# The first load of a layer norm cut into three strided transfers, with a 64-byte write per DMA engine between the first two

## The chip, the cores and the metric

One core of one Trainium2 chip. The metric is the device time of one execution in microseconds, as a median over executions. All runs told here are of the state "fast", with a granted clock of 1.0. Ratios are the mean time of one kernel's fast runs over that of the other's fast runs of the same rounds on the same chip, so they are not quite the ratio of the medians that are quoted beside them.

## The reference

Condensed:

```python
def reference(x, residual, gamma, beta, eps):        # x, residual: 16 x 1024 x 512, float32
    z = x + residual
    mean = np.mean(z, axis=-1, keepdims=True)
    var = np.var(z, axis=-1, keepdims=True)
    return (gamma * (z - mean) / np.sqrt(var + eps) + beta).astype(np.float32)
```

Two tensors of 33.5 MB are read and one is written: 100.7 MB through the DMA engines.

## The kernel before

Every row is 512 floats (2 KB). A partition holds 128 rows, and `x32+16` in the plan means: rows 32 to 47 of each of the 128 partitions. GpSimd adds x and the residual into `rbuf`, ScalarE makes mean and variance, VectorE normalizes into `zbuf`, and the result is stored from there. All large transfers are issued by SyncE on one queue, in the order of the plan. The first two are moved ahead of the barrier at which the engines meet at the start.

```python
PLAN = """
x0+8 r0+8 x8+8 r8+8 x16+16 r16+16 x32+16 r32+16 x48+16
o0+16 r48+16 o16+16 x64+16 r64+16 x80+16 o32+16 r80+16
x96+16 r96+16 o48+8 o56+8 r112+8 x112+8 r120+8 x120+8
o64+16 o80+16 o96+16 o112+8 o120+4 o124+4
"""
EARLY = 2
# ... buffers, semaphores, gamma and beta ...
    def move(out, in_, s):
        i = nc.sync.dma_start(out=out, in_=in_).then_inc(s, 16)
        if len(first) < EARLY:
            first.append(i.ins)
    for kind, lo, n in moves:
        if kind == "x":
            # ... wait until the buffer's rows have been stored ...
            move(part(zbuf, Z_ROWS, lo, n), dram(xf, lo, n), sx[loads_x.index((lo, n))])
        elif kind == "r":
            # ... wait until the buffer's rows have been used ...
            move(part(rbuf, R_ROWS, lo, n), dram(rf, lo, n), sr[loads_r.index((lo, n))])
        else:
            if lo + n > seen:
                nc.sync.wait_ge(s_out, lo + n)
                seen = lo + n
            move(dram(of, lo, n), part(zbuf, Z_ROWS, lo, n), so[stores.index((lo, n))])
# ... GpSimd waits for x and r (16 on each load's semaphore), then adds ...
# ... at the end, `first` is moved into the opening, ahead of the start barrier ...
```

Of the kernel before, what the change touches and what calls it, by code (L numbers as in the profile page):

```python
# [8 lines left out]
FP32 = mybir.dt.float32  # L9
# [5 lines left out]
Z_ROWS = 64  # L15
# [16 lines left out]
Z_TURNS = Z_ROWS // TURN  # L32


EARLY = 2


@with_exitstack
def kernel(
# [9 lines left out]
    nc = tc.nc  # L49
    P = nc.NUM_PARTITIONS  # L50
    xf = x.flatten_outer_dims()
    rf = residual.flatten_outer_dims()
    of = out.flatten_outer_dims()
# [14 lines left out]
    def of_kind(kind):  # L68
        found = [(lo, n) for k, lo, n in moves if k == kind]
        assert sum(n for _, n in found) == total  # L70
        return found

    def dram(t, lo, n):

        b0 = lo - lo % BLOCK
        v = t[P * b0 : P * (b0 + BLOCK), :].rearrange("(p j) d -> p j d", p=P)
        return v[:, lo - b0 : lo - b0 + n, :].rearrange("p a b -> p (a b)")

    zbuf = nc.alloc_sbuf_tensor("zbuf", [P, Z_ROWS * D], FP32)
    rbuf = nc.alloc_sbuf_tensor("rbuf", [P, R_ROWS * D], FP32)  # L80
    gb_row = nc.alloc_sbuf_tensor("gb_row", [1, 2 * D], FP32)
    ones = nc.alloc_sbuf_tensor("ones", [1, P], FP32)
    eps_t = nc.alloc_sbuf_tensor("eps_t", [P, 1], FP32)
    nm, ssq, std, rstd = (
        nc.alloc_sbuf_tensor(name, [P, R_ROWS], FP32) for name in ("nm", "ssq", "std", "rstd")
# [11 lines left out]
    def sem(name):  # L97
        s = nc.alloc_semaphore(name)
        sems.append(s)
        return s  # L100

    loads_x, loads_r, stores = of_kind("x"), of_kind("r"), of_kind("o")
    sx = [sem(f"sx{c}") for c in range(len(loads_x))]
    sr = [sem(f"sr{c}") for c in range(len(loads_r))]
    s_gb = [sem(f"gb{k}") for k in range(2)]
    s_const = sem("const")
    s_pe = sem("pe")
    s_sum, s_mean, s_ssq, s_std = (
        [sem(f"{name}{j}") for j in range(R_TURNS)] for name in ("sum", "mean", "ssq", "std")
# [7 lines left out]
    def part(buf, size, lo, n):  # L117
        assert lo % size + n <= size
        return buf[:, (lo % size) * D : (lo % size + n) * D]
# [17 lines left out]
    first = []  # L137

    def move(out, in_, s):
        i = nc.sync.dma_start(out=out, in_=in_).then_inc(s, 16)  # L140
        if len(first) < EARLY:
            first.append(i.ins)

    gone = 0
    for kind, lo, n in moves:
        if kind == "x":
            while gone < len(stores) and stores[gone][0] < lo + n - Z_ROWS:
                nc.sync.wait_ge(so[gone], 16)
                gone += 1
            move(part(zbuf, Z_ROWS, lo, n), dram(xf, lo, n), sx[loads_x.index((lo, n))])  # L150
        elif kind == "r":
            if lo + n > R_ROWS:
                last = (lo + n - R_ROWS) // TURN - 1
                nc.sync.wait_ge(s_rstd[last % Z_TURNS], last // Z_TURNS + 1)
            move(part(rbuf, R_ROWS, lo, n), dram(rf, lo, n), sr[loads_r.index((lo, n))])
        else:
            if lo + n > seen:
                nc.sync.wait_ge(s_out, lo + n)
                seen = lo + n
            move(dram(of, lo, n), part(zbuf, Z_ROWS, lo, n), so[stores.index((lo, n))])  # L160
# [9 lines left out]
    landed = {"x": 0, "r": 0}  # L170
    lo = 0
    for n in ADDS:
        for key, loads, s in (("x", loads_x, sx), ("r", loads_r, sr)):
            while landed[key] < len(loads) and loads[landed[key]][0] < lo + n:
                nc.gpsimd.wait_ge(s[landed[key]], 16)  # L175
                landed[key] += 1
        z = part(rbuf, R_ROWS, lo, n)
        nc.gpsimd.tensor_tensor(  # L178
            out=z, in0=part(zbuf, Z_ROWS, lo, n), in1=z, op=ALU.add
        ).then_inc(s_sum[lo // TURN % R_TURNS], 1)  # L180
        lo += n
# [131 lines left out]
```

## Time and profile before

| | before |
|---|---|
| time, median of 3 runs | 238.48 us (238.36 to 238.83) |
| span of the profiled run | 236.7 us |
| busy: VectorE, ScalarE, GpSimd | 75%, 78%, 61% |
| the one large queue | 99.4% of 16 DMA engines' span |

The last row is the one to read: the 16 DMA engines are the bound. The lines of the profile stand in the prediction. The timeline of the start shows when SyncE issues transfers (start, duration, both in us), the timeline of GpSimd when it can add for the first time, which is when the first loads of x and of the residual have landed on every engine:

```profile
0.00 0.38 SPq L140 DMA_DIRECT2D zbuf<-in_x_dram  x1
...
0.43 0.42 SPq L140 DMA_DIRECT2D rbuf<-in_residual_dram  x1
1.92 0.33 SPq L140 DMA_DIRECT2D zbuf<-in_x_dram  x1
```

```profile
12.29 4.49 POOL L178 TENSOR_TENSOR rbuf<-zbuf,rbuf 128x2048 f32<-128x2048 f32 x1 [11.85 <-DMA rbuf<-in_residual_dram]
```

### The profile page before, as it was taken

To read this page: it belongs to the slowest core of one execution; us is meant where nothing else is said; L and a number is where in the kernel's file an instruction comes from. 1 tells how busy PE (TensorE), PEld (TensorE's weight loads), DVE (VectorE), ACT (ScalarE), POOL (GpSimd) and SP (SyncE) were. 2 spreads that over 40 slices of the span, in tenths; PEclk is the share of its full clock that TensorE was granted. 3 is DMA by queue.
4 is the path that set the end of the run, shared out by engine and by line. 5 is a ranking of instruction groups with operands and counts; after the bars stand their busy time and mean duration, and the time that the engine had idled before them with its cause. 6 is when DMAs were issued, how large, how long until landed. Compare 5 with 4: busy or idle time off the path is not lost.

```text
span 236.7 us, 1000 instructions
## 1 busy us (share of the span) xinstructions
PE 3.8 (2%) x4; PEld 1.2 (0%) x4; DVE 177.2 (75%) x290; ACT 183.8 (78%) x545; POOL 144.0 (61%) x36
## 2 busy tenths in 40 slices
PE   0600000000000000000000000000000000000000
PEld 0100000000000000000000000000000000000000
DVE  0001999629999999599980999809999999999950
ACT  2019997299999996999909998099999999999600
POOL 0098920999799307993079920899799798800000
DMA  8999999999999999999999999999999999999997
GB/s 310 443 426 432 426 443 443 443 443 443 410 388 443 443 443 432 426 393 432 443 443 443 443 438 421 415 421 432 429 424 435 426 432 440 439 432 443 438 390 324
DMA packets 4469, 100.68 MB, mean 425 GB/s; under 512 B 498, under 2 KB 498, under 8 KB 500
## 3 DMA queue, kind: packets, MB, share of 16 engines
q1 hardware_dynamic: 4464, 100.67, 99.4%
q14 instruction: 1, 0.01, 0.0%
q10 hardware_dynamic: 4, 0.00, 0.0%
HBM read 67.11 MB, written 33.55 MB: 425 GB/s over the span
## 4 chain that ended last, share of the span: by engine, by line
ACT 48%; DMA 35%; POOL 6%; DVE 4%; issue 1%; SPq 1%; ACTq 0%; DVEq 0%; POOLq 0%
DMA rbuf<-in_residual_dram 35%; ACT junk_s L211 25%; ACT junk_m L201 21%; POOL rbuf L178 6%; DVE zbuf L239 3%; ACT std L220 2%; DVE zbuf L253 1%; SPq L140 1%; DVE rstd L247 0%; ACTq L194 0%; DVEq L231 0%; POOLq L175 0%; ACTq L199 0%; ACTq L195 0%
## 5 line engine op out<-in xcount | busy, mean ns | idle before, releaser
L178 POOL TENSOR_TENSOR rbuf<-zbuf,rbuf 128x2048 f32<-128x2048 f32 x32 | 143.7, 4521 | 62.2 <-DMA rbuf<-in_residual_dram 60.0
L239 DVE SCALAR_TENSOR_TENSOR zbuf<-rbuf,nm,gamma_p 128x512 f32<-128x512 f32 x128 | 87.1, 743 | 47.8 <-ACT std L220 47.8
L201 ACT ACTIVATE junk_m<-rbuf 128x512 f32<-128x512 f32 x128 | 74.2, 580 | 34.0 <-POOL rbuf L178 33.7
L211 ACT ACTIVATE junk_s<-rbuf,nm 128x512 f32<-128x512 f32 x128 | 88.8, 694 | 1.0
L253 DVE SCALAR_TENSOR_TENSOR zbuf<-zbuf,rstd,beta_p 128x512 f32<-128x512 f32 x128 | 87.1, 744 | 1.1
L211 ACT ACTIVATION_READ_ACCUMULATOR junk_s<-rbuf,nm 128x1 f32 x128 | 23.9, 187 | 0.0
L201 ACT ACTIVATION_READ_ACCUMULATOR junk_m<-rbuf 128x1 f32 x128 | 23.8, 186 | 0.0
L220 ACT ACTIVATE std<-ssq,eps_t 128x4 f32<-128x4 f32 x32 | 9.5, 297 | 1.0
L247 DVE RECIPROCAL rstd<-std 128x4 f32<-128x4 f32 x32 | 5.5, 171 | 0.0
L192 ACT ACT_TABLE_LOAD x1 | 1.3, 1283 | 2.7 <-PEq L60 2.7
L131 PE MATMUL gamma_p<-gb_row,ones 1*128 1x512 f32 x2 | 2.0, 1122 | 6.6 <-DMA gb_row<-in_gamma_dram 6.6
L131 PE MATMUL beta_p<-gb_row,ones 1*128 1x512 f32 x2 | 1.9, 1056 | 0.0
L126 DVE MEMSET ones<- 1x128 f32 x1 | 0.2, 165 | 2.0 <-PEq L60 2.0
L131 PEld LDWEIGHTS beta_p<-gb_row,ones 1*128 1x128 f32 x2 | 0.7, 332 | 1.0 <-DMA gb_row<-in_beta_dram 0.5
L131 PEld LDWEIGHTS gamma_p<-gb_row,ones 1*128 1x128 f32 x2 | 0.5, 306 | 6.6 <-issue 6.6
L294 POOL MEMSET const-float32-0.0<- 128x1 f32 x1 | 0.1, 98 | 0.2 <-issue 0.2
L294 POOL MEMSET const-bfloat16-1.0<- 128x1 bf16 x1 | 0.1, 101 | 0.0
L294 POOL MEMSET const-uint8-127<- 128x1 uint8 x1 | 0.1, 101 | 0.0
L294 POOL MEMSET const-float32-1.0<- 128x1 f32 x1 | 0.1, 98 | 0.0
L127 DVE MEMSET eps_t<- 128x1 f32 x1 | 0.1, 59 | 0.0
## 6 DMA issues: line engine op xcount, KB each, us to landing
zbuf<-in_x_dram SPq DMA_DIRECT2D x6, 4096.0 KB, 28.9
rbuf<-in_residual_dram SPq DMA_DIRECT2D x6, 4096.0 KB, 21.2
out_dram<-zbuf SPq DMA_DIRECT2D x6, 4096.0 KB, 31.0
zbuf<-in_x_dram SPq DMA_DIRECT2D x4, 2048.0 KB, 14.9
rbuf<-in_residual_dram SPq DMA_DIRECT2D x4, 2048.0 KB, 14.0
out_dram<-zbuf SPq DMA_DIRECT2D x3, 2048.0 KB, 22.5
out_dram<-zbuf SPq DMA_DIRECT2D x2, 1024.0 KB, 10.0
gb_row<-in_gamma_dram ACTq DMA_DIRECT2D x1, 2.0 KB
```

Source lines behind the costliest of these rows:

```text
L126: nc.vector.memset(ones[:, :], 1.0).then_inc(s_const, 1)
L131: nc.tensor.matmul(dest[:, :], ones[:, :], gb_row[:, k * D : (k + 1) * D], start=True, stop=True).then_inc(s_pe, 1)
L140: i = nc.sync.dma_start(out=out, in_=in_).then_inc(s, 16)
L178: nc.gpsimd.tensor_tensor(out=z, in0=part(zbuf, Z_ROWS, lo, n), in1=z, op=ALU.add).then_inc(s_sum[lo // TURN % R_TURNS], 1)
L192: act.preload_act_table_set("sqrt_and_others")
L201: i = act.activation(out=junk_m[k][:, :], in_=part(rbuf, R_ROWS, r, 1), func=ACT.Identity, scale=-inv_d, accum_out=column(nm, r),)
L211: i = act.activation(out=junk_s[k][:, :], in_=part(rbuf, R_ROWS, r, 1), func=ACT.Square, bias=column(nm, r), accum_out=column(ssq, r),)
L220: act.activation(out=column(std, rows[0], TURN), in_=column(ssq, rows[0], TURN), func=ACT.Sqrt, bias=eps_t[:, 0:1], scale=inv_d,).then_inc ...
L239: dve.scalar_tensor_tensor(out=part(zbuf, Z_ROWS, r, 1), in0=part(rbuf, R_ROWS, r, 1), scalar=column(nm, r), in1=gamma_p[:, :], op0=ALU.ad ...
L247: dve.reciprocal(out=column(rstd, rows[0], TURN), in_=column(std, rows[0], TURN)).then_inc(s_rstd[j], 1)
L253: i = dve.scalar_tensor_tensor(out=z, in0=z, scalar=column(rstd, r), in1=beta_p[:, :], op0=ALU.mult, op1=ALU.add,)
L294: nc = _bacc.Bacc("TRN2", target_bir_lowering=False, num_devices=1)
```

## The change

The evident intent: engines should start on a short first piece, and the cost of the first write to the output, a stall near 69 us, should be paid at the start, where the engines wait for their first read anyway. The residual's first load falls out of the opening, as the list of early instructions is filled by the pieces. The diff, with line positions left out and two declarations (the scratch tile and the two semaphores) cut:

```diff
-EARLY = 2
+TOUCH = 16
+FIRST = [(0, 4), (2, 4), (1, 2)]
 ...
-        if len(first) < EARLY:
+        if len(first) < len(FIRST) + 3:
             first.append(i.ins)
 ...
-            move(part(zbuf, Z_ROWS, lo, n), dram(xf, lo, n), sx[loads_x.index((lo, n))])
+            for a, step in FIRST if lo == 0 else [(0, 1)]:
+                move(
+                    part(zbuf, Z_ROWS, lo, n)[a::step, :],
+                    dram(xf, lo, n)[a::step, :],
+                    sx[loads_x.index((lo, n))],
+                )
+                if len(first) == 1:
+                    first.append(nc.vector.memset(zeros[:, :], 0.0).then_inc(s_zero, 1).ins)
+                    first.append(nc.sync.wait_ge(s_zero, 1).ins)
+                    move(dram(of, 0, 1)[::8, 0:TOUCH], zeros[::8, :], s_touch)
 ...
             if lo + n > seen:
+                if lo == 0:
+                    nc.sync.wait_ge(s_touch, 16)
                 nc.sync.wait_ge(s_out, lo + n)
 ...
-                nc.gpsimd.wait_ge(s[landed[key]], 16)
+                pieces = len(FIRST) if key == "x" and landed[key] == 0 else 1
+                nc.gpsimd.wait_ge(s[landed[key]], 16 * pieces)
```

The pieces are partitions 0, 4, 8 ... (32 of them), 2, 6, 10 ... (32) and all odd ones (64): two, two and four packets of 16 KB for each engine.

## The prediction

> **What bounds the kernel now.** I began with the page's second and third parts, because they say at once whether an engine or the transfers carry the time.
>
> ```profile
> DMA  8999999999999999999999999999999999999997
> GB/s 310 443 426 432 426 443 443 443 443 443 410 388 443 443 443 432 426 393 432 443 443 443 443 438 421 415 421 432 429 424 435 426 432 440 439 432 443 438 390 324
> q1 hardware_dynamic: 4464, 100.67, 99.4%
> HBM read 67.11 MB, written 33.55 MB: 425 GB/s over the span
> ```
>
> The reader is to see that all loads and stores go through one queue and that its packets fill 99.4% of the 16 DMA engines' span of 236.7 us; only the first and the last slice (5.9 us each) are weaker. VectorE (75%), ScalarE (78%) and GpSimd (61%) all idle more. The page's chain of work that ended last puts 48% on ScalarE, but it ends with the last compute instruction, not with the last store. The timeline of the end shows the difference:
>
> ```profile
> 216.75 11.81 SPq L140 DMA_DIRECT2D out_dram<-zbuf  x3
> 225.48 2.72 DVE L253 SCALAR_TENSOR_TENSOR zbuf<-zbuf,rstd,beta_p 128x512 f32<-128x512 f32 x4
> ```
>
> Compute ends at 225.48 + 2.72 = 228.20 us, the last store is issued at 228.2 us, and the transfers run on to 236.7 us. I put the queue's issue times beside the landing times of the trace's records: from the fourth load on, every transfer is issued at least 5 us before the queue would run dry. So the kernel is a continuous stream with a head (before the first packet) and a few stalls inside; a stall that goes shortens the whole by its length, until some 5 us are won.
>
> Next I looked for the stalls: windows of half a microsecond to two. Their last two columns count packets that start in the window, as a share of 16 engines and as GB/s.
>
> ```profile
> 0.00:1.00 1.00, 0.00 (x0) 0.00 (x0) 0.00 (x0) 0.00 (x0) 0.20 (x4) 1.00 0.00 0
> 1.00:1.50 0.50, 0.00 (x0) 0.00 (x0) 0.00 (x0) 0.00 (x0) 0.00 (x0) 1.00 2.47 524
> 1.50:2.00 0.50, 0.00 (x0) 0.00 (x0) 0.00 (x0) 0.00 (x0) 0.00 (x0) 1.00 0.00 0
> 2.00:2.50 0.50, 0.00 (x0) 0.00 (x0) 0.17 (x2) 0.00 (x0) 0.00 (x0) 1.00 0.90 360
> ...
> 68.00:69.00 1.00, 0.00 (x0) 0.00 (x0) 0.99 (x2) 0.97 (x5) 1.00 (x1) 1.00 1.63 524
> 69.00:70.00 1.00, 0.00 (x0) 0.00 (x0) 0.83 (x2) 0.80 (x4) 1.00 (x2) 1.00 0.00 0
> 70.00:71.00 1.00, 0.00 (x0) 0.00 (x0) 1.00 (x2) 1.00 (x4) 1.00 (x1) 1.00 1.22 524
> ```
>
> The first stall is at the head. All 16 engines start their first 16 KB packet between 1.02 and 1.49 us, and none starts another until 2.25 us. In the packet records those first packets took 1.02 to 1.37 us; a later 16 KB packet takes 0.61 us. That is 0.62 us lost per engine. The second is at 69 us: no packet starts for a whole microsecond, although a 32 KB packet normally takes 1.21 us and those in flight began at 68.45 to 68.86. They took 1.32 to 1.91 us, a mean excess of 0.41 us and at most 0.69. They are the last packets of a load of x, and what stands behind them in the queue is the first store of the kernel. No later change from load to store has such a stall (at the second, near 88 us, the worst packet is 0.06 us over), nor has the first read of the residual, near 6.6 us. Elsewhere the excess is a few hundredths. So one stall of about 0.41 us belongs to the first write to the output, once.
>
> **What the Trainium skill says.** "DMA: Bandwidth & Descriptors", section "Specifications", gives about 0.6 us to the first byte on this path and 512 B as the least size at line rate; the trace has 1.02 us from the issue to the first packet, and a 2 KB packet (gamma) of 84 ns against 76 ns for that share of a 16 KB one. Its section "Queues, rings and completion order" says that each DMA engine takes a queue's descriptors in ring order and that a completion increment lands after that engine's earlier writes; this agrees with the stall at 69 us, which holds up what stands ahead of the store as well. "SBUF — State Buffer", section "Door 1: The DMA port swizzle", lists which partitions share one of 16 ports: partitions 0, 4, 8 ... 124 reach all 16, two each, while 32 adjacent ones would reach only 8. Before has whole 128-partition transfers only, so no run here shows that yet. No page I found names a cost of the first write.
>
> **The change, part by part.** Bytes and compute do not change; on VectorE one memset is added ahead of the start barrier, and the other engines keep their instructions in order.
>
> 1. Removed: the stall at the first store, if the small write has paid for it. -0.41 us by the mean; the end is set by the slowest engine, so -0.3 to -0.6.
> 2. Added: the small write, 16 packets of 64 B, one for each engine. Warm I estimate 0.1 us per engine at most (the 2 KB packet took 0.084). Cold it brings the same first-write stall of 0.3 to 0.6 us. What counts is whether that overlaps the cold first read. Queue order is: two packets of x per engine, the write, the other six packets. With 0.43 us per issue, as now, the write is issued at 0.43 us, and with the 1.02 us from issue to packet it could be seen by the engines near 1.5 us, when they are still in the stalled first packet (until 2.3 to 2.7). So there is a window of about 1 us for hiding. I take the cost as half hidden: +0.2 us.
> 3. Smaller first piece. Before, the 128 descriptors of the first load reached the engines spread over 0.47 us (1.02 to 1.49). 32 descriptors should be spread over a quarter of that, about 0.12 us, so the mean start moves up by 0.17 us; the cold read behind it may swallow some. -0.1 to -0.2, I take -0.1.
> 4. Two more loads' issues and one wait. Four issues end at about 1.75 us instead of two at 0.86; the start barrier, the residual's first load and gamma's come about 0.9 us later. First residual at about 2.8 us: the queue then still holds x until about 6.5 us (the eight packets per engine), so nothing runs dry. GpSimd's first add waits for the residual until 12.29 us, and everything moved by the barrier is done by then. The memset takes 0.06 to 0.17 us by the two VectorE memsets after the barrier, and the wait on it lies behind the first issue of 0.38 us. +0.0.
> 5. Three more completions per engine at 9 ns a record: +0.03 us. The wait before the first store (issued at 45.5 us) was over 40 us earlier: 0.
>
> Sum: -0.41 + 0.2 - 0.1 + 0.03 = about -0.3 us, from 238.48 to 238.2 us.
>
> **Rivals.** *The stall is only moved.* If the write blocks the engine after the cold read instead of beside it, part 2 costs 0.4 and the sum is -0.1: 238.4 us. For it speaks that at 69 us the queue did not run past the cold write. *All hidden, and the head shorter too*: part 2 costs 0.05, part 3 brings -0.2; -0.55, 237.9 us. For it speaks the 1 us in which the first read stalls anyway. *Strided pieces are slow*: if engines and ports do not pair up as with 128 partitions, the eight packets per engine (4.9 us) could take half as long again: +2.5 us, 241 us. The stride of 4, which gives every port two rows, speaks against. *The stall at 69 us is no first touch but the turn from reading to writing a large store*: then it stays and the write is pure cost, +0.1: 238.6 us. The missing stall at the second store speaks against it.
>
> **Range and chances.** All but the third rival lie between 237.9 and 238.6; the three runs of before differ by 0.47 us among themselves. Predicted 238.15 us, range 237.6 to 238.8. A gain of 2% would be 4.8 us; the whole head plus the stall are under 3 us, so faster has 1%. Slower by 2% needs the strided rival at its worst: 1%.
>
> **What would show it.** In the changed kernel: no window near 69 us without starting packets, and its packets back at 1.21 us (part 1); the first packets starting within about 0.15 us of one another (3); the six later packets of x at 0.61 us each (the strided rival dead); a second stall between 2 and 4 us if the cost was moved, none if it was hidden (2); the residual's first issue near 2.8 us with no gap near 6.5 us (4). I am wrong if the stall near 69 us is still there, if pieces two and three run slower than 0.61 us a packet, or if the queue runs dry before the residual.

## The result, and the profile after

The changed kernel takes 240.4 us (240.0 to 241.22, 6 runs) against 238.27 us of before (6 runs): a ratio of 1.0092, interval 1.0071 to 1.0113. It is slower by some 2.1 us, outside the predicted range of 237.6 to 238.8. Second and third part of its page:

```profile
DMA  7999999999999999999999999999999999999997
GB/s 253 404 434 458 434 439 434 423 434 423 439 351 434 434 428 434 428 428 439 439 434 417 439 434 434 439 428 439 401 436 423 431 434 450 424 439 434 425 413 303
q1 hardware_dynamic: 4528, 100.67, 98.9%
```

The queue is still the bound, and the first slice is the one that has fallen most (253 against 310 GB/s). The timeline of its start, SyncE's issues:

```profile
0.00 0.56 SPq L145 DMA_DIRECT2D zbuf<-in_x_dram  x1
...
0.61 0.57 SPq L145 DMA_DIRECT2D out_dram<-zeros  x1
1.23 1.23 SPq L145 DMA_DIRECT2D zbuf<-in_x_dram  x2
3.75 0.35 SPq L145 DMA_DIRECT2D rbuf<-in_residual_dram  x1
```

Each of the new issues takes about 0.6 us instead of 0.4, and the second piece of x is issued at 1.23 us. Then windows of half a microsecond (the last two columns are the share and the GB/s of packets that start in the window), first of the changed kernel, then of before:

```profile
1.00:1.50 0.50, 0.00 (x0) 0.00 (x0) 0.00 (x0) 0.00 (x0) 0.00 (x0) 1.00 1.36 328
1.50:2.00 0.50, 0.00 (x0) 0.00 (x0) 0.00 (x0) 0.00 (x0) 0.00 (x0) 1.00 0.51 131
...
3.00:3.50 0.50, 0.00 (x0) 0.00 (x0) 0.00 (x0) 0.00 (x0) 0.00 (x0) 1.00 0.76 264
3.50:4.00 0.50, 0.00 (x0) 0.00 (x0) 0.15 (x2) 0.00 (x0) 0.00 (x0) 1.00 0.85 295
4.00:4.50 0.50, 0.00 (x0) 0.00 (x0) 0.02 (x2) 0.00 (x0) 0.00 (x0) 1.00 0.75 262
4.50:5.00 0.50, 0.00 (x0) 0.00 (x0) 0.00 (x0) 0.44 (x1) 0.00 (x0) 1.00 0.76 295
```

```profile
3.00:3.50 0.50, 0.00 (x0) 0.00 (x0) 0.00 (x0) 0.50 (x1) 0.00 (x0) 1.00 0.86 360
3.50:4.00 0.50, 0.00 (x0) 0.00 (x0) 0.00 (x0) 0.49 (x1) 0.00 (x0) 1.00 1.16 492
4.00:4.50 0.50, 0.00 (x0) 0.00 (x0) 0.00 (x0) 0.00 (x0) 0.00 (x0) 1.00 1.18 492
4.50:5.00 0.50, 0.00 (x0) 0.00 (x0) 0.00 (x0) 0.00 (x0) 0.00 (x0) 1.00 0.92 393
```

Between 3 and 5 us the changed kernel moves 262 to 295 GB/s where before moves 360 to 492. I counted the packets in flight from the trace's packet records: before has 15 or 16 at every moment from 2.6 us on; the changed kernel has 16 at 3.0 us, 7 at 3.36 us, and is not back at 15 for good before 5.2 us. (The records do not name the engine; a packet counts as in flight from its start to its end.) That is 0.56 us of idle time per engine. In addition packets between 3 and 8 us are long (a 16 KB packet takes over the usual 0.61 us), by 0.51 us per engine in sum. Both together are most of what the mean engine loses: the 16 landings of the residual's first load are 1.20 us later on average. It is unequal: the residual's first load lands on the fastest engine at 12.37 us (before: 11.76), on the slowest at 14.05 (before: 12.15). GpSimd waits for the slowest:

```profile
14.19 4.49 POOL L195 TENSOR_TENSOR rbuf<-zbuf,rbuf 128x2048 f32<-128x2048 f32 x1 [13.76 <-DMA rbuf<-in_residual_dram]
```

So 1.90 us are lost by 14 us, on the slowest engine. The difference is the same at the load that lands near 61 us (62.69 against 60.81). The next place is the first store. Windows of the changed kernel there:

```profile
68.00:69.00 1.00, 0.00 (x0) 0.00 (x0) 0.96 (x4) 1.00 (x3) 1.00 (x1) 1.00 1.04 295
69.00:70.00 1.00, 0.00 (x0) 0.00 (x0) 1.00 (x2) 1.00 (x5) 1.00 (x1) 1.00 1.06 262
70.00:71.00 1.00, 0.00 (x0) 0.00 (x0) 0.87 (x2) 0.97 (x3) 1.00 (x1) 1.00 0.72 262
```

The stall that the small write should have removed is still there and wider: three microseconds at 262 to 295 GB/s instead of one empty one. Its packets are long by 1.16 us per engine in sum, against 0.42 in before. The load ahead of the store lands on the slowest engine at 73.69 us against 70.94: 2.75 us behind. Later 0.6 us come back (last landing 238.76 against 236.62). Perhaps the engine that is last at the end is not the one that was last in the middle; the records do not name engines, so this is not shown. The sum, by construction: 1.90 + 0.85 - 0.61 = 2.14 us.

### The profile page after: what moved, and what is told of

Same layout as the page of the kernel before. It is cut to its first block, busy times and chain, and to the rows that moved or that the text cites. A ratio compares the mean times of both kernels' runs of the same rounds, so it can differ in the third digit from the quotient of the medians.

```text
span 238.8 us, 1005 instructions
## 1 busy us (share of the span) xinstructions
PE 3.7 (2%) x4; PEld 1.1 (0%) x4; DVE 177.3 (74%) x291; ACT 183.7 (77%) x545; POOL 144.0 (60%) x36
## 4 chain that ended last, share of the span: by engine, by line
ACT 48%; DMA 35%; POOL 6%; DVE 4%; issue 1%; SPq 1%; ACTq 0%; DVEq 0%; POOLq 0%
DMA rbuf<-in_residual_dram 35%; ACT junk_s L228 25%; ACT junk_m L218 21%; POOL rbuf L195 6%; DVE zbuf L256 3%; ACT std L237 2%; SPq L145 1%; DVE zbuf L270 1%; DVE rstd L264 0%; ACTq L211 0%; DVEq L248 0%; POOLq L192 0%; ACTq L216 0%; ACTq L212 0%
```

## The experiments

All medians and ratios; the last columns are readings from the traces: when GpSimd's first add starts, the idle time per engine between 2.6 and 6.6 us, and the sum per engine by which packets are long around the first store. Each kernel has one trace, so the last three columns are single readings; differences of some 0.4 us in the last one may be chance (e1 and e16 below).

| run | time us | before us | ratio (95%) | first add | idle | first store |
|---|---|---|---|---|---|---|
| before | | 238.27 | 1 | 12.29 | 0.01 | 0.42 |
| changed kernel | 240.40 | 238.27 | 1.0092 (1.0071 to 1.0113) | 14.19 | 0.56 | 1.16 |
| e1_pieces_only | 239.14 | 238.21 | 1.0036 (1.0021 to 1.0051) | 13.57 | 0.24 | 0 |
| e2_touch_only | 238.34 | 238.21 | 1.0004 (0.9991 to 1.0017) | 12.38 | 0.01 | 0.56 |
| e3_mid_pieces | 238.22 | 238.21 | 1.0002 (0.9989 to 1.0015) | | 0.01 | 0.38 |
| e4_touch_mid | 238.21 | 238.21 | 1.0001 (0.9988 to 1.0014) | | 0 | 0.44 |
| e5_touch_last | 239.38 | 238.04 | 1.0064 (1.0051 to 1.0077) | 13.88 | 0.25 | 0.02 |
| e6_store_early | 238.13 | 238.04 | 1.0016 (1.0002 to 1.0031) | | 0 | 0.38 at 58 us |
| e7_two_halves | 239.23 | 238.04 | 1.0055 (1.0043 to 1.0067) | 13.87 | 0.13 | 0.21 |
| e8_skew | 239.79 | 238.04 | 1.0076 (1.0062 to 1.0091) | | 0.01 | 0 |
| e9_after_store_early | 240.54 | 238.16 | 1.0099 (1.0084 to 1.0115) | 13.77 | 0.48 | 0.81 at 59 us |
| e10_residual_opening | 240.31 | 238.16 | 1.0097 (1.0081 to 1.0112) | 14.83 | 0.44 | 0.90 |
| e11_column_pieces | 240.08 | 238.16 | 1.0081 (1.0067 to 1.0095) | 13.74 | 0.33 | 0.73 |
| e12_second_load | 238.14 | 238.16 | 0.9998 (0.9983 to 1.0014) | 12.43 | 0 | 0.43 |
| e13_small_read | 240.32 | 238.10 | 1.0095 (1.0078 to 1.0111) | 14.39 | 0.35 | 0.40 |
| e14_large_early_write | 239.73 | 238.10 | 1.0068 (1.0053 to 1.0084) | | 0.01 | 0.82 at 29 us |
| e15_long_first_piece | 238.23 | 238.10 | 1.0011 (0.9998 to 1.0025) | 12.37 | 0.01 | 0.51 |
| e16_pieces_residual | 239.50 | 238.10 | 1.0067 (1.0052 to 1.0083) | 13.82 | 0.22 | 0.52 |
| e17_pause | 239.97 | 238.09 | 1.0084 (1.0070 to 1.0098) | 13.97 | 0.37 | 1.03 |

All results were correct. The diffs below show the lines that matter; declarations and the matching changes of waits and of the list of early instructions are left out.

### Which part does it? e1 and e2

**e1_pieces_only**, from the changed kernel:

```diff
-                if len(first) == 1:  ... memset, wait, small write ...
-                if lo == 0:  nc.sync.wait_ge(s_touch, 16)
```

> The first load of x in the same three strided pieces, no small write, no memset and no wait. Before is 238.3 us, the changed kernel 240.4. Theory A (the strided pieces do the harm: their descriptors reach the engines late, and the slowest engine sets the end): most of the 2.1 us stays, 239.6 to 240.4 us, and between 3 and 5.5 us fewer than 16 engines have a packet in flight. Theory B (the small write does it: the engines wait for their first write to the output): back to 238.1 to 238.5 us, all 16 engines busy from 2.3 us on.

239.14 us: neither. The pieces alone cost 0.9 us, under the range of theory A. Its engines run dry too, but later: windows of this run.

```profile
3.00:3.50 0.50, 0.00 (x0) 0.00 (x0) 0.17 (x2) 0.00 (x0) 0.00 (x0) 1.00 1.42 524
3.50:4.00 0.50, 0.00 (x0) 0.00 (x0) 0.00 (x0) 0.09 (x1) 0.00 (x0) 1.00 1.07 459
4.00:4.50 0.50, 0.00 (x0) 0.00 (x0) 0.00 (x0) 0.50 (x1) 0.00 (x0) 1.00 0.95 197
4.50:5.00 0.50, 0.00 (x0) 0.00 (x0) 0.00 (x0) 0.50 (x1) 0.00 (x0) 1.00 1.15 262
```

From 3 to 4 us the rate is full, as the second piece (issued at 0.60 us) is there in time; from 4 us it falls to 197: the third piece (1.22 us) is not. Twelve packets that start between 4.28 and 5.01 us, when engines resume, are also long: 0.77 to 1.67 us instead of 0.61.

**e2_touch_only**, from the changed kernel:

```diff
-FIRST = [(0, 4), (2, 4), (1, 2)]
+FIRST = [(0, 1)]
```

> The first load of x whole, the small write behind it on the same queue, the residual's first load behind the start barrier as in the changed kernel. Theory A: 238.2 to 238.6 us, the head as in before (first load landed near 7.3 us). Theory B: 239.5 us or more, with a gap of 1 to 2 us on the engines behind the write, near 7 us. For the stall near 69 us: if it is a first touch of the output that the small write pays for, it is gone and the time is 0.3 us lower; if it is as large as before (0.4 us per engine), the small write buys nothing.

238.34 us, so theory A: no gap, and the write costs nothing that the interval can tell from zero. The stall at the first store is as it was (0.56 us per engine): the small write buys nothing either. In this run as in before, no packet starts between 69 and 70 us:

```profile
69.00:70.00 1.00, 0.00 (x0) 0.00 (x0) 0.82 (x3) 0.80 (x3) 1.00 (x2) 1.00 0.00 0
```

The two parts together cost more (2.1 us) than the sum of each alone (0.9 and 0.1). How much more is less sure: a second kernel with pieces and no write (e16) lost 1.4 us.

### Is it the strides or the write itself, in the middle of the stream? e3 and e4

**e3_mid_pieces** and **e4_touch_mid**, both from before:

```diff
# e3: the load of rows 16 to 31 of x in the three strided pieces
-            move(part(zbuf, Z_ROWS, lo, n), dram(xf, lo, n), sx[...])
+            for a, step in [(0, 4), (2, 4), (1, 2)] if lo == 16 else [(0, 1)]:
+                move(part(zbuf, Z_ROWS, lo, n)[a::step, :], dram(xf, lo, n)[a::step, :], sx[...])
# e4: behind the same load
+            if lo == 16:
+                # memset of zeros and its wait
+                move(dram(of, 0, 1)[::8, 0:TOUCH], zeros[::8, :], s_touch)
```

> The kernel before with the load of rows 16 to 31 of x (4 MB, 32 KB per partition) in the same three strided pieces; it is issued near 3 us and its packets run from about 22 to 32 us, so its descriptors are there long before. Theory A (late descriptors): no cost, 238.2 to 238.5 us, packets at 1.21 us. Theory C (a strided piece itself moves slower, as engines and ports or memory banks collide): packets over 1.3 us, the load takes 1 to 5 us longer than its 9.7 us, 239.3 us or more.

> The kernel before with the small write of 64 bytes per engine put in the queue behind the load of rows 16 to 31 of x, so that it runs near 31 us between full-size packets. Theory A: within 0.1 us of before, 238.2 to 238.5. Theory B (a first write stops an engine): a gap of 0.4 to 2 us near 31 us. The stall near 69 us: gone if the small write is what it waits for (then the sum is 238.3 or less), unchanged at 0.4 us per engine if not.

238.22 and 238.21 us, both as before, so theory A in both. A window over the strided load in e3, and the same of before:

```profile
22.00:32.00 10.00, 0.00 (x0) 0.00 (x0) 8.98 (x15) 9.87 (x31) 9.02 (x2) 1.00 0.97 419
```

```profile
22.00:32.00 10.00, 0.00 (x0) 0.00 (x0) 9.05 (x16) 9.87 (x31) 9.02 (x2) 1.00 0.97 419
```

In mid-stream a strided piece moves at full rate: theory C falls. In e4 the stall near 69 us stays (0.44 us): a first touch of the output by 64 bytes per engine does not pay for it.

### Where the write stands, and how long the first piece is: e5, e7, e15

**e5_touch_last**, from the changed kernel, puts the write behind all three pieces:

```diff
-                if len(first) == 1:
+                if len(first) == len(FIRST):
```

> The three strided pieces first, then the small write, everything else as in the changed kernel (240.4 us; pieces alone gave 239.1, the small write alone 238.3). Theory A (the write costs by its place: it takes an issue slot of 0.6 us between pieces while the engines have only two packets each, so the second piece comes a slot later): 238.9 to 239.4 us, as with the pieces alone. Theory D (pieces and write together bring something of their own, wherever the write stands): 240 us or more, and the stall near 69 us is again over 1 us per engine.

239.38 us, at the upper end of theory A's range, 1.3 us over before: between the two kernels with pieces alone (0.9 in e1, 1.4 in e16) and under the changed kernel. The stall at the first store is 0.02 us here, so pieces and write together do not bring it wherever the write stands.

**e7_two_halves**, from the changed kernel:

```diff
-FIRST = [(0, 4), (2, 4), (1, 2)]
+FIRST = [(0, 2), (1, 2)]
```

> As the changed kernel, but the first load in two strided halves of 64 partitions (four packets per engine, not two) with the small write between them. Theory A (the descriptors of the next piece come late): the first half now lasts until about 4.3 us, so most of the gap is covered; 238.5 to 239.2 us. If strided pieces cost by their number of issues alone: about 239.5. If the pair of pieces and write does it whatever the sizes: 240 or more.

239.23 us, just outside the range of theory A and under the other two. Four packets per engine in the first piece instead of two halve the loss (1.2 us instead of 2.1), though only 0.13 us per engine are idle, from 4.4 us on; the larger part is that packets are long (0.73 us per engine between 3 and 8 us).

**e15_long_first_piece**, from e11 below: two pieces along the row, 12 KB and 4 KB per partition.

```diff
-FIRST = [(0, 2), (2, 2), (4, 4)]
+FIRST = [(0, 6), (6, 2)]
```

> Two pieces cut along the row, 12 KB and 4 KB per partition, the small write between them: the first piece keeps every engine busy until about 5.3 us. Late descriptors predict no idle engines before 9 us and 238.0 to 238.6 us. If a small write between two pieces of the first load costs whatever the pieces' length: 239.5 or more.

238.23 us, as predicted. The write still stands between two pieces of the first load, and nothing is lost. The rate from 1.0 to 6.5 us, in this run, then in before and in the changed kernel:

```profile
1.00:6.50 5.50, 0.00 (x0) 0.00 (x0) 0.17 (x2) 1.28 (x1) 0.00 (x0) 1.00 0.98 376
```

```profile
1.00:6.50 5.50, 0.00 (x0) 0.00 (x0) 0.17 (x2) 1.28 (x1) 0.00 (x0) 1.00 1.02 382
```

```profile
1.00:6.50 5.50, 0.00 (x0) 0.00 (x0) 0.17 (x2) 1.28 (x1) 0.00 (x0) 1.00 0.88 313
```

69 GB/s less over 5.5 us are 0.38 MB, or 0.9 us of the full rate of some 430 GB/s, on average over the engines.

### Place, shape, and kind of the transfer between: e10 to e13

**e12_second_load** does all of it on the second load of x; the first loads stay whole and early.

```diff
-            for a, step in FIRST if lo == 0 else [(0, 1)]:
+            for a, step in FIRST if lo == 8 else [(0, 1)]:
```

> The same three pieces and small write on the second load of x instead of the first; the first loads of x and the residual stay whole and ahead of the barrier. Late descriptors: 10 us of packets stand in the queue by then, so nothing is lost, 237.9 to 238.5 us and the stall of 0.4 us at the first store unchanged. If pieces and write cost by themselves: 239 or more.

238.14 us: nothing lost. The same pieces and write cost 2.1 us at the head and 0 behind 10 us of queued packets.

**e11_column_pieces**, from the changed kernel, keeps the bytes of each piece but takes all 128 partitions each time:

```diff
-FIRST = [(0, 4), (2, 4), (1, 2)]
+FIRST = [(0, 2), (2, 2), (4, 4)]
-                    part(zbuf, Z_ROWS, lo, n)[a::step, :],
-                    dram(xf, lo, n)[a::step, :],
+                    part(zbuf, Z_ROWS, lo + a, m),
+                    dram(xf, lo + a, m),
```

> The changed kernel with its three pieces cut along the row instead of over the partitions: 128 partitions of 4 KB, 4 KB and 8 KB, the same bytes per engine and piece (64, 64 and 128 KB per engine in all three taken as 2, 2 and 4 packets of 16 KB), the small write in the same place. If a partial, strided transfer is what is slow to issue (0.56 to 0.59 us, whole ones 0.33 to 0.43) and to reach the engines: 238.4 to 239.2 us and hardly a gap. If any short first transfer starves the engines, as the next transfer's descriptors come too late: 240 us or more, with idle engines from 3 to 5.5 us as in the changed kernel.

240.08 us: the second reading. A short first transfer starves the engines in both shapes; that it covers part of the partitions is not the point. (The expectation has the bytes per engine doubled: pieces of 0.5, 0.5 and 1 MB are 32, 32 and 64 KB for each of 16 engines.)

**e10_residual_opening**, from the changed kernel, issues the residual's first load ahead of the barrier again:

```diff
-        if len(first) < len(FIRST) + 3:
+        if len(first) < len(FIRST) + 4:
```

> The changed kernel with the residual's first load also issued ahead of the start barrier, as before had it. The queue is not empty near 9 us in the changed kernel, so the theory of late descriptors says no gain: 240.0 to 240.8 us. If the residual's later issue is part of the loss: 239 to 239.7. It also is a second look at the first store of the changed kernel: a stall of about 1 us per engine if it is the kernel's own.

240.31 us: no gain, so the later residual (3.75 us instead of 0.43) is not part of the loss. The stall at the first store is 0.90 us per engine.

**e13_small_read**, from the changed kernel:

```diff
-                    move(dram(of, 0, 1)[::8, 0:TOUCH], zeros[::8, :], s_touch)
+                    move(zeros[::8, :], dram(xf, 0, 1)[::8, 0:TOUCH], s_touch)
```

> The changed kernel with the 64 bytes per engine read from x into the scratch tile instead of written to the output; order, waits and everything else are the same. If only the slot between the pieces counts: 240.2 to 240.8 us again, with 0.7 us or more per engine at the first store. If the write to the output is what makes the first store's stall large: 239.2 to 239.7 us, head as bad as in the changed kernel, but 0 to 0.4 us at the first store.

The time says the first (240.32 us), the stall at the first store is 0.40 us, which is what the second had said; packets were long by another 0.4 us in this trace between 33 and 50 us. What is plain: no write to the output is needed for the loss.

### The delay without the transfer: e17, and without both: e16

**e17_pause**, from the changed kernel: no small transfer, but a longer memset (128 by 1024) whose end SyncE awaits before the second piece.

```diff
-TOUCH = 16
+TOUCH = 1024
-                    move(dram(of, 0, 1)[::8, 0:TOUCH], zeros[::8, :], s_touch)
```

> The three strided pieces without the small transfer, but with a wait in its place, on a memset of 128 by 1024 elements (0.91 us in an earlier trace, so done at about 1.1 us): the second piece is issued near 1.2 us, as in the changed kernel (1.23), instead of 0.60. If the later issue is the additional loss: 240.0 to 240.7 us, as in the changed kernel. If it is the transfer itself, its hand-out to 16 engines: 239.0 to 239.6 us, as with the pieces alone.

239.97 us, ratio 1.0084, just under the first range and far from the second. The timeline shows the memset that holds the pieces back (it ends at 1.27 us; the trace has the second piece at 1.30), and the window from 1.0 to 6.5 us has nearly the rate of the changed kernel:

```profile
0.36 0.91 DVE L162 MEMSET zeros<- 128x1024 f32 x1 [0.36 <-issue]
```

```profile
1.00:6.50 5.50, 0.00 (x0) 0.00 (x0) 0.44 (x3) 1.28 (x1) 0.00 (x0) 1.00 0.92 319
```

Pieces with a later second issue and no small transfer lose 1.9 us of the 2.1, where pieces alone lost 0.9 (e1) or 1.4 (e16). So the delay by itself brings most of what the small write adds, and within the intervals it may be all: the harm of the small write is the 0.6 us that it takes of SyncE's time.

**e16_pieces_residual**, from e1: the residual's first load ahead of the barrier.

```diff
-        if len(first) < len(FIRST):
+        if len(first) < len(FIRST) + 1:
```

> The three strided pieces without the small write, and the residual's first load ahead of the barrier again. Second look at the case without the write: head loss as with the pieces alone (1.0 to 1.3 us on the slowest engine), stall at the first store 0 to 0.2 us per engine, 238.8 to 239.4 us. If the stall is 0.4 us or more here, its absence in the first trace was an accident.

239.50 us, a little over the range. The stall at the first store is 0.52 us: by what I had written, its absence in e1 was an accident of that trace, and no theory may rest on it. The same caution holds for the other single readings of that stall.

### The stall at the first store: e6, e8, e9, e14

**e6_store_early**, from before, and **e9_after_store_early**, from the changed kernel, have the same edit:

```diff
-x0+8 r0+8 x8+8 r8+8 x16+16 r16+16 x32+16 r32+16 x48+16
-o0+16 r48+16 ...
+x0+8 r0+8 x8+8 r8+8 x16+16 r16+16 x32+16 r32+16 o0+16
+x48+16 r48+16 ...
```

> The kernel before with the first store put ahead of the load of rows 48 to 63 of x, so that it runs near 61 us instead of 71. If the stall of 0.4 us per engine belongs to the first store, it moves to about 58 to 60 us and leaves 68 us; if it belongs to that load or to that time, it stays near 68. Time in both cases 238.0 to 238.7 us.

> The changed kernel with the first store put ahead of the load of rows 48 to 63 of x, which moved the stall of the kernel before to 58 us and cost nothing there. If the large stall of the changed kernel (1.15 us per engine near 69 us in its trace) belongs to its first store and comes in every execution: it is near 59 us now, again about 1 us, and the time stays at 240 to 240.8. If that stall was an accident of the one trace: 0 to 0.4 us, and 239.3 to 240.

In e6 the stall moved to 57 to 60 us and left 68 us; windows of e6:

```profile
58.00:59.00 1.00, 0.00 (x0) 0.00 (x0) 1.00 (x2) 1.00 (x5) 1.00 (x1) 1.00 0.46 164
59.00:60.00 1.00, 0.00 (x0) 0.00 (x0) 1.00 (x3) 1.00 (x3) 0.57 (x1) 1.00 1.15 393
```

It belongs to the first store. In e9 it moved too and was 0.81 us, and the time stayed at 240.54: the larger stall of the changed kernel was no accident.

**e8_skew**, from before: eight small loads that only some engines take.

```diff
+            for k in range(8) if lo == 8 else ():
+                move(skew[8 * k : 8 * k + 8, :], dram(xf, 0, 2)[8 * k : 8 * k + 8, :], s_skew[k])
```

> The kernel before with eight additional loads of 8 partitions by 4 KB, which only some of the DMA engines take (half of them by the count of partitions), behind the second load of x: a skew of about 1.25 us between engines (8 times 0.155 us) with no strided piece and no small write. If the larger stall near 69 us in the changed kernel comes from the skew of its engines: here too it is 0.8 us per engine or more, and the time 239.8 to 241. If not: 0.4 us as in before, and 239.3 to 239.8 us, the skew and no more.

239.79 us, as the second reading had it; the stall was not 0.4 us as it said, but gone. Yet its engines were as unequal (1.59 us between the first and the last landing near 61 us, 1.67 in the changed kernel). In this trace unequal engines alone did not enlarge it.

**e14_large_early_write**, from e4: 128 by 4 KB of zeros instead of 64 bytes per engine.

```diff
-TOUCH = 16
+TOUCH = 1024
-                move(dram(of, 0, 1)[::8, 0:TOUCH], zeros[::8, :], s_touch)
+                move(dram(of, 0, 2), zeros[:, :], s_touch)
```

> The kernel before with a write of 128 by 4 KB of zeros (0.5 MB, 1.2 us of the queue by its rate) to the output behind the load of rows 16 to 31 of x. If the stall of 0.4 us belongs to the first write of any real size, it shows near 31 us and is gone near 69 us: 239.3 to 239.5 us. If it is still near 69 us, an earlier write does not pay for it: 239.3 to 239.8 us, and the trace decides.

239.73 us. The windows show the stall ahead of the early write, and none at the first store:

```profile
29.00:30.00 1.00, 0.00 (x0) 0.00 (x0) 1.00 (x3) 1.00 (x4) 1.00 (x1) 1.00 0.96 262
30.00:31.00 1.00, 0.00 (x0) 0.00 (x0) 1.00 (x2) 0.97 (x5) 1.00 (x1) 1.00 0.89 262
...
69.00:70.00 1.00, 0.00 (x0) 0.00 (x0) 1.00 (x2) 1.00 (x5) 1.00 (x1) 1.00 1.21 524
```

So in this trace an earlier large write took the stall over, and only moved it. What speaks for this is the stall ahead of the early write; that there is none at the first store proves little, as e1, e5 and e8 have none there either without such a write. The run is 1.6 us slower: 1.2 us for its own bytes, and the stall at its new place was 0.82 us per engine instead of 0.4.

No version beat the kernel before.

## Why the prediction was wrong, point by point

**What bounds the kernel: right.** The queue is the bound in every run, and what the slowest engine loses at the head is still there at the end.

**Part 1, the stall goes (-0.41 us): wrong.** The prediction took it for a first touch of the output that any write pays for. It belongs to the first store (e6), but 64 bytes per engine do not pay for it (e2: 0.56, e4: 0.44 us). Of the writes tried only one of half a megabyte took it over (e14, one trace). The order of descriptors and increments, with which the prediction found the stall in agreement, does not say why packets ahead of a store should be long. In the changed kernel the term was +0.85 us on the slowest engine.

**Part 2, the small write (+0.2 us, taken as half hidden): wrong in what it costs.** As a transfer it cost nothing that shows (e2, e4): in the changed kernel it landed on all engines 0.1 to 0.2 us behind the first piece, and no stall of a first write showed there. Its cost was its place in SyncE's order (e17).

**Part 3, the engines start earlier (-0.1 us): wrong.** I scaled the 0.47 us over which the first packets start by the number of descriptors. The first packets of the short piece started at 1.33 to 2.23 us instead of 1.02 to 1.49. The later start is in all traces: the first packet of a strided first piece came at 1.32 to 1.35 us, that of a first transfer over all partitions at 1.00 to 1.02. The spread is not: whole first loads in other runs reach as late (1.01 to 1.81 us in e2, 1.00 to 2.16 in e6), a strided one was as close as 1.33 to 1.63 (e9). So the 0.47 us of one trace was nothing to scale.

**Part 4, "so nothing runs dry" (+0.0 us): this is the step that failed most.** I used the 1.02 us from the first issue to its first packet and 0.43 us per issue for all that follows (the new issues took 0.56 to 0.59 us, and the residual's came at 3.75 us, not 2.8), and asked only whether the queue would run dry at the residual. It did not there (e10). It ran dry between the pieces. Two packets per engine keep an engine busy until about 3.1 us; the second piece, issued at 1.23 us, was not with every engine by then, and some were without a packet until about 5 us. The runs agree on this: with a second piece 0.6 us earlier the gap starts at 4.4 us (e1), with four packets in the first piece likewise (e7), and with a first piece that lasts until 5.2 us there is none (e15). In before, the first load lasts until 6.5 us, which hid the delay from view: nothing in the trace before showed when a second transfer reaches the engines, only that it was in time. In place of 0.0 the term is 1.9 us on the slowest engine in the changed kernel. Empty engines are only a part of it: packets between 3 and 8 us are also long, by 0.5 us per engine in the changed kernel and 0.7 to 0.8 in e1 and e7, more there than the idle time. This comes with the gap, 0.5 to 0.8 us in all ten traces whose queue ran dry and under 0.05 in all others, but why is not explained.

**The rivals.** "Strided pieces are slow", 241 us, came nearest in time and was wrong in its cause: e3 has strided pieces at full rate, e11 has whole partitions and loses as much. "Only moved" and "all hidden" both rested on part 1. The fourth, that the stall stays and the write is pure cost, was right about the stall (e2, e4), and 238.34 us in e2 does not contradict its 238.6; it had no term for the pieces.

**The range and the chances.** "Within 2%" held. The range of 1.2 us was too narrow because all rivals but one shared part 4, with its untested 1.02 us.

**What stays open.** Why the stall at the first store is 0.7 to 1.2 us in five of the six traces of kernels with a first piece of 0.5 MB and a second issued at 1.0 to 1.3 us (e13, with 0.40, is the exception), and 0 to 0.6 in the others. Skew between engines alone did not do it in e8, the small write is not needed for it (e17: 1.03). What the first store waits for was not found. Nor was it shown what between the issue and the engines takes the time at the head; shown is only that what was issued at 1.0 to 1.9 us is with the last engine by about 5 us.

## What to carry to other kernels

Where a queue of transfers is the bound, the first transfer has to be long enough to keep every engine busy until the next ones reach all engines; here that took until about 5 us. A first transfer of 2 MB (16 KB per partition) or 1.5 MB (e15) cost nothing, one of 1 MB 1.2 us (e7) and one of 0.5 MB 0.9 to 2.4 us, and most of that was still missing at the end of the run. A time from issue to first packet, read where the queue was empty, must not be used for the second transfer; a trace in which the queue is always full does not show it at all. A tiny transfer between short ones at the head is not free: it costs the issuing engine's time for those behind it. Behind a long first load (e2, e15), or with 10 us of packets in the queue (e12), the same transfer cost nothing.

## What the Trainium skill lacked or had wrong

- "DMA: Bandwidth & Descriptors", section "Specifications", gives some 0.6 us to the first byte and does not say from where it counts. Here the first packet started 1.00 to 1.02 us after the start of a whole first issue, which is 0.6 us after its end (the issue took 0.38 us), and 1.32 to 1.35 us after the start of a strided one (0.54 to 0.57 us long). The last engine got its first packet later, at 1.49 us in before and up to 2.2 us elsewhere. A second or third short transfer, issued at 1.0 to 1.9 us, was not with the last engine before 4.6 to 5.4 us. The page has no number for a second transfer.
- The same page, section "Rules for kernel authors", advises against two transfers to disjoint halves because they serialize. At the head of a queue it is worse: two strided halves with a small write between them were 1.2 us slower than one transfer (e7; no run has the halves without the write). In mid-stream, three pieces cost nothing (e3, e12).
- No page that I found has the stall ahead of the first store of size, at most once per execution: 0.4 us per engine in before, 0 to 1.2 in other runs, moved by the order of transfers (e6) and by an earlier write of 0.5 MB (e14), not by 64 bytes per engine (e2, e4).
- No page that I found says how long an issue holds the issuing engine by the transfer's shape and by what was issued before it. Here a first issue took 0.38 us over 128 partitions and 0.54 to 0.57 over 32 or 64, and the small write 0.55 to 0.59. It is no rule for all partial transfers: those over 8 partitions took 0.28 to 0.31 us behind one another (e8), and whole ones right behind the small write took 0.57 to 0.58 (e15, e4).
